# S5 layer of a decoder trunk: recurrence steps issued in two parts, and five small pieces of work put at other places

## The chip, the core and the metric

The kernel runs on one core of a Trainium2 chip. Five engines of that core work side by side and meet at semaphores: TensorE (PE in the profile, with its weight loads as PEld), VectorE (DVE), ScalarE (ACT), GpSimd (POOL) and SyncE (SP), which here only issues transfers from HBM. The metric is the time of one execution in microseconds (us); before the change it was 2031.78 us, the median of 3 runs that lay between 2030.18 and 2032.72 us. One further execution was recorded by the profiler; every duration below comes from that one.

## What is computed

A two-layer decoder trunk in float32 over 256 tokens of width 2048. Layer 0 mixes tokens with an S5 state-space mixer, layer 1 with sliding-window attention; a SwiGLU feed-forward network follows each. The change lies in layer 0's mixer alone:

```python
def s5_mixer(u, a_re, a_im, log_step, b_re, b_im, c_re, c_im, d_skip, w_glu):
    dt = exp(log_step)[:, None]
    lb = exp((a_re + i a_im) * dt)                 # 128 groups x 64 complex states
    q  = (lb - 1) / (a_re + i a_im)
    bb = q[..., None] * (b_re + i b_im)            # 64 states x 16 channels per group
    bu = einsum('lgc,gpc->lgp', u, bb)
    s[l] = lb * s[l-1] + bu[l]                     # the recurrence, over 256 tokens
    y = real(einsum('lgp,gcp->lgc', s, c)) + d_skip * u
    g = gelu(y)
    gl = g @ w_glu                                 # 2048 x 4096
    return gl[..., :2048] * sigmoid(gl[..., 2048:])
```

Its input `u` is the RMS norm of `x` with weights `norm_mix[0]`.

## The kernel before, in words

**Tiling.** The 256 tokens are cut into 64 chunks (`NK`) of 4 tokens (`L`). Inside a chunk the effect of the tokens on each other is a small matrix product on TensorE (`own_tokens`, with the matrices `M`); from chunk to chunk runs the recurrence, 63 values of the state, so 62 steps. The 128 groups form 64 pairs; pairs are split in two halves `hf` = 0 and 1, each with its own state tile `V0` or `V1` (`V` in the profile) of 64 chunks x 64 numbers per partition (real and imaginary parts of 32 columns). The two recurrences don't depend on each other.

**Ahead of the recurrence** (the first 56 us of the profile), TensorE and ScalarE go back and forth: `turned_x` transposes a block of `X` (TensorE, `px`) and ScalarE copies it (`xt`); `tokens` does the same with the normed input (`pu`, `U`); `added` multiplies both (`pv`), and `kept` copies the product into `V0` or `V1` on ScalarE. Blocks are numbered (t, b) with t = 0 to 3, b = 0 to 3; t = 0, 1 fill `V0`, and t = 2, 3 fill `V1`. The norm needs its weights spread over the partitions: two matrix products `gb` with `sel`; they are used by `scaled` (tile `xs`), which VectorE computes after the norm's scale `r` is known. The sum of squares behind `r` passes TensorE as the product `rb`. `pl` is another small set of products shortly before it (the powers of lb, by pair).

**The recurrence.** `step(hf)` is three VectorE instructions: a product of 4 x 32 numbers per partition (line 573) and two sums of 2 x 32 (lines 576 and 578), each on what the one before wrote. Early steps of half 0 are called by `lead`; the main loop (line 851 on) then calls a step of half 0 and, once `reached[0]` is more than `LEAD` = 20 ahead, one of half 1. When half 0 is through, half 1 goes on alone by `more`. ScalarE copies finished states into `St`, in cuts that end at chunks 28, 52, 60 and 64.

**After the recurrence.** `outputs(q)` (line 798) multiplies the states `St[q]` and adds them to `own_tokens(q)` (line 776) in the banks `py`; ScalarE applies GELU (`activated`, line 806), TensorE transposes (`turned`, tile `pt`), ScalarE rounds to the high part (line 820) and VectorE subtracts for the low part (line 821) of the tile `gt`. Quarters q = 0 and 2 belong to half 0, and 1 and 3 to half 1. `end(0, 2)` and `end(1, 3)` do this for two quarters.

**The weights.** `w_glu` and all later matrices come as pieces of 512 x 512 numbers, 1 MB, loaded by SyncE's queue into `raw`, of which there are two buffers. `W.high(i)` makes the rounded high part on ScalarE (line 122), `W.low(i)` the rest, on VectorE (line 127) unless GpSimd is named. A raw buffer is free for piece i+2 once both parts of piece i are made. A piece takes 24 products on TensorE (lines 922 to 924: high x high, low, and low x high, for 4 row blocks and 2 token blocks). `early_piece` runs the first four pieces between the S5 stages.

**What sets the order.** Each engine takes its instructions in one fixed order. Calls wrapped in `pin`, and the calls between `V.on = True` and `V.on = False` for that engine, stay in the order in which the program is written; the others are placed by a scheduler when the program is built. Waits on semaphores are inserted at the same time, wherever an instruction reads or overwrites what another one writes. They are tracked by stretches of memory, so a wait may stand between two instructions whose numbers interleave but are not the same.

Of the kernel before, what the change touches and what calls it, by code (L numbers as in the profile page):

```python
# [9 lines left out]
F32 = mybir.dt.float32  # L10
# [7 lines left out]
P = 128  # L18
# [29 lines left out]
def bc(ap, axis, n):  # L48

    v = ap.unsqueeze(axis)  # L50
    shape = list(v.shape)
    shape[axis] = n
    return v.to_broadcast(shape)
# [3 lines left out]
def kernel(  # L57
# [22 lines left out]
    def bank(shape, name="ps"):  # L80
        return ps.tile(shape, F32, tag="ps", name=nm(name))
# [112 lines left out]
    def s5(early_piece):  # L194
# [3 lines left out]
        with st:  # L198
# [21 lines left out]
            def rows(g2):  # L220
                return slice(g2 * NS, (g2 + 1) * NS)
# [70 lines left out]
            S.copy(Bn[:, 2], Bn[:, 0])  # L292


            gb = [bank([P, 512], "gb") for _ in range(2)]
            for hf in range(2):
                PE.matmul(gb[hf], sel.rearrange("p k h -> p (k h)"), nrow[:, 512 * hf : 512 * hf + 512],
                          start=True, stop=True)


            V.on = False
            n_small = [0]

# [75 lines left out]
            nr, t, u, w = (sp.tile(sh, F32, name=f"q{i}") for i in range(4))  # L379
            V.on = True  # L380
            V.tensor_scalar(nr, LP[:, 0, 0], -1.0, None, ALU.add)
            PL.tensor_tensor(u, LP[:, 0, 1], aim, op=ALU.mult)
            PL.tensor_tensor(t, nr, are, op=ALU.mult)
            PL.tensor_tensor(w, nr, aim, op=ALU.mult)
            PL.tensor_tensor(t, t, u, op=ALU.add)
            PL.tensor_tensor(u, LP[:, 0, 1], are, op=ALU.mult)
            PL.tensor_tensor(q_[:, 0], t, iv, op=ALU.mult)
            PL.tensor_tensor(u, u, w, op=ALU.subtract)
            PL.tensor_tensor(q_[:, 1], u, iv, op=ALU.mult)


            ssq = sp.tile([P, L], F32, name="ssq")

# [6 lines left out]
            def turned_b(o, i, evict):  # L400
                f = 0 if o is B1 else 1
                b = Bn[:, f : f + 2].rearrange("p r s c -> p (r s) c")
                pt = bank([P, 4, G])
                for c in range(4):
                    PE.transpose(pt[:, c], b[:, :, 4 * i + c], ident)
                evict(o[:, :, 4 * i : 4 * i + 4], pt.rearrange("p c g -> p g c"))
# [9 lines left out]
            turned_b(B1, 3, S.copy)  # L416
            turned_b(B2, 0, negated)
            squares(2)
            turned_b(B2, 1, negated)
            for i in (2, 3):  # L420
                turned_b(B2, i, lambda o, v: V.tensor_scalar(o, v, sgn[:, 1:2], None, ALU.mult))


# [7 lines left out]
            for l in range(L):  # L431
                for ri in range(2):
                    for g2 in range(2):
                        PE.matmul(pl[rows(g2), l, ri], LP[:, l, ri], ident[:, g2::2], start=True, stop=True)
            LRs = sp.tile([P, 3, G], F32, name="LRs")
            S.copy(LRs, LR)

# [11 lines left out]
            def last_token(t):  # L449
                S.copy(X[t][:, :, :, 3].rearrange("p (h a) g c -> p h (a g) c", h=2), of_groups(B1, t))  # L450
# [69 lines left out]

            tokens(0, 0)
            tokens(0, 1)
            last_token(1)

            early.close()
            lp = st.enter_context(tc.tile_pool(name="s5late", bufs=1))
# [2 lines left out]
            def turned_x(t, b):  # L529
                px = bank([P, 4, P], "px")  # L530
                for i in range(4):
                    PE.transpose(px[:, i], X[t][:, 4 * b + i].rearrange("p g j c -> p (g j c)"), ident)
                xt[t, b] = lp.tile([P, 4, 2, NS], F32, tag="xt", name=nm("xt"), bufs=4)
                S.copy(xt[t, b].rearrange("p a r s -> p a (r s)"), px)
# [11 lines left out]
            def kept(t, b, copy):  # L546
                p0 = 16 * (b // 2) + 8 * (t % 2) + 4 * (b % 2)
                copy(Vt[t // 2][:, 1:, :, p0 : p0 + 4], pvs[t, b].rearrange("p r a k -> p k r a")[:, : NK - 1])
# [14 lines left out]
            def step(hf, parts=1, keep=lambda ins: ins):  # L563

                reached[hf] += 1
                k = reached[hf]
                n = 32 // parts
                ws, pr = scan[hf][:, 0], scan[hf][:, 1]
                vs = []
                for i in range(parts):  # L570
                    part = slice(n * i, n * (i + 1))
                    t_ = pr[..., part]
                    keep(V.tensor_tensor(t_, ws[..., part], bc(Vt[hf][:, k - 1, :, part], 1, 2), op=ALU.mult))  # L573
                    vs.append((Vt[hf][:, k, :, part], t_))
                for v, t_ in vs:
                    V.tensor_tensor(v, v, t_[:, 0], op=ALU.add)  # L576
                for v, t_ in vs:
                    V.tensor_tensor(v, v, t_[:, 1, ::-1], op=ALU.add)  # L578

            def lead(n):  # L580
                for i in range(n):
                    step(0)

            for t in (2, 3):
                real_parts(t)
            PL.tensor_copy(drows[:, :, 3], drow.rearrange("a (g c) -> a g c", g=2))

            def imag_and_tokens(t):
                for j in (2, 1):
                    imag(t, j)  # L590
                for j in (2, 1):
                    token(t, j)
                imag(t, 0)
                token(t, 0)

            turned_x(0, 0)
            turned_x(0, 1)
            imag_and_tokens(1)
            added(0, 0)
            kept(0, 0, S.copy)  # L600
# [36 lines left out]
            PL.tensor_tensor(Cq[:, :, 0], Cq[:, :, 0], c2[:, :, 1], op=ALU.subtract)  # L637
            PL.tensor_tensor(Cq[:, :, 1], Cq[:, :, 1], c2[:, :, 0], op=ALU.add)

            lead(4)  # L640
            last_token(2)
            tokens(2, 0)
# [2 lines left out]
            turned_x(2, 1)  # L645
            added(2, 0)
            kept(2, 0, S.copy)
            turned_x(2, 2)
            added(2, 1)
            kept(2, 1, S.copy)  # L650
# [19 lines left out]
            lead(3)  # L670
            added(3, 2)
            kept(3, 2, S.copy)

            pc = bank([P, PAIRS], "pc")
            PE.transpose(pc, drows.rearrange("a g j c -> a (g j c)"), ident[:PAIRS, :PAIRS])
            dcol = lp.tile([P, PAIRS], F32, name="dcol")
            S.copy(dcol, pc)
            dd = lp.tile([P, PAIRS, GC], F32, name="dd")
            PL.tensor_tensor(dd, bc(dcol, 2, GC), bc(idm, 1, PAIRS), op=ALU.mult)
            added(3, 3)  # L680
            kept(3, 3, S.copy)
            lead(2)
            W.high(0, pin)
            W.low(0, pin, PL)
            for e in (V, S, PL, PE):
                e.on = False

# [163 lines left out]
                    pin(copied(q, cuts[cuts.index(k1) - 1], k1))  # L851

            while reached[0] < NK - 1:
                step(0)
                if reached[0] + 1 in cuts:
                    copies((0, 2), reached[0] + 1)
                if reached[0] + 1 == cuts[2]:

                    M[1] = kernels(lags, pin)
                    for q in (0, 2):  # L860
                        own_tokens(q)
                if reached[1] + LEAD < reached[0] < NK - 1:
                    step(1)
            W.high(1, pin)

            def more(n):

                for i in range(min(n, NK - 1 - reached[1])):
                    step(1, keep=pin)

            rest = cuts[1:]

# [10 lines left out]
            early_piece(gt, 0, 0, last)  # L883
            W.low(2, pin)
            W.high(3, pin)
            W.low(3, pin, PL)
            for q in (1, 3):
                St[q] = big([P, 2, 16, NK], "St")
            copies_so_far()
# [5 lines left out]
            own_tokens(1)  # L895
            W.high(4, pin)
            last = end(1, 3, lambda: own_tokens(3))
            early_piece(gt, 1, 2, last)
            W.low(4, pin)
            W.high(5, pin)  # L900
# [406 lines left out]
```

## Time and profile before

| | |
|---|---|
| median of 3 runs | 2031.78 us (2030.18 to 2032.72) |
| the profiled execution's own time | 2030.9 us |
| its span, first to last instruction | 2029.1 us |
| mean granted TensorE clock | 0.993 of full speed |
| S5's recurrence: half 1's first step starts | 56.55 us |
| half 0's last step is done, half 1 goes on alone | about 98.4 us |
| first `outputs(1)` product, right after half 1's last states | 124.61 us |
| TensorE's idle time after 180 us, in 1849 us | 12.9 us |

The profiled execution is 0.88 us shorter than the median. The span leaves out 1.8 us ahead of and behind the instructions. The first rows of the table show the shape: some 130 us of S5, in which no engine works all the time, and then some 1900 us of products, in which TensorE hardly ever stops. In a row of a timeline the first number is the start in us from the span's start, the second the duration; a bracket gives the idle time just before the row, and what ended it.

### The profile page before, as it was taken

What the parts mean: (1) busy time and instruction counts of PE and PEld (TensorE: products, weight loads), DVE (VectorE), ACT (ScalarE), POOL (GpSimd) and SP (SyncE); (2) the same over time, 40 slices, a digit from 0 to 9 for tenths busy, and PEclk for the clock granted to TensorE, in tenths of its full rate; (3) what the DMA queues carried; (4) which work ended last, traced back from release to release, by engine and by line L of the source; (5) the groups of instructions that cost most, each with busy time, mean ns of one, the idle gap of its engine ahead of it and who ended that gap; (6) DMA issues with size and microseconds to landing.
All of it is one profiled execution on the core that took longest, in us unless ns stands there. A gap on an engine that the chain in (4) does not pass through costs nothing.

```text
span 2029.1 us, 25100 instructions
## 1 busy us (share of the span) xinstructions
PE 1984.3 (98%) x10640; PEld 1638.7 (81%) x10640; DVE 1088.9 (54%) x1343; ACT 860.1 (42%) x871; POOL 103.7 (5%) x77
## 2 busy tenths in 40 slices
PE   7699999999999999999999999999999999999998
PEld 6578888888888888888887778888888888888886
DVE  8955454445544544454567775544454445444445
ACT  6554444443344334333445454544333343334333
POOL 6850000000000000000000000000000000000000
PEclk9899999999999999999999999999999999999999
DMA  4037666565555655556555334556555655555564
GB/s 128 23 111 233 198 198 194 186 194 192 187 188 188 199 193 187 187 192 200 178 191 166 106 125 146 186 188 193 194 192 187 188 191 193 195 186 188 190 201 148
DMA packets 183317, 360.62 MB, mean 178 GB/s; under 512 B 10403, under 2 KB 10467, under 8 KB 183077
## 3 DMA queue, kind: packets, MB, share of 16 engines
q1 hardware_dynamic: 182192, 355.56, 54.4%
q8 instruction: 83, 1.36, 0.3%
q10 hardware_dynamic: 580, 2.14, 0.3%
q0 software_dynamic: 432, 1.33, 0.2%
q14 instruction: 30, 0.24, 0.0%
HBM read 356.90 MB, written 2.10 MB: 177 GB/s over the span
## 4 chain that ended last, share of the span: by engine, by line
PE 91%; DVE 6%; ACT 1%; DMA 1%; issue 1%; POOL 0%; DVEq 0%; ACTq 0%
PE acc L922 29%; PE acc L924 29%; PE acc L923 28%; DVE scan L573 1%; DVE w L127 1%; PE tr L1061 1%; DVE V L578 1%; DVE V L576 1%; DMA raw<-in_s_w_glu_dram 1%; PE pv L210 1%; PE tr L966 1%; PE po L1208 1%; PE tr L1197 0%; PE py L798 0%; ACT sc L1181 0%
## 5 line engine op out<-in xcount | busy, mean ns | idle before, releaser
L127 DVE TENSOR_TENSOR w<-raw,w 128x2048 fp32r<-128x2048 f32 x330 | 757.1, 2295 | 828.3 <-ACT w L122 828.3
L122 ACT ACTIVATE w<-raw 128x2048 fp32r<-128x2048 f32 x332 | 636.2, 1916 | 979.4 <-PE acc L924 873.6
L922 PE MATMUL acc<-w,xT 128*128 128x512 f32 x1568 | 612.8, 391 | 0.0
L924 PE MATMUL acc<-w,xT 128*128 128x512 f32 x1568 | 611.3, 390 | 0.0
L923 PE MATMUL acc<-w,xT 128*128 128x512 f32 x1568 | 610.6, 389 | 0.0
L924 PEld LDWEIGHTS acc<-w,xT 128*128 128x128 f32 x1568 | 294.3, 188 | 62.2 <-issue 1.0
L922 PEld LDWEIGHTS acc<-w,xT 128*128 128x128 f32 x1568 | 294.4, 188 | 61.3 <-issue 1.3
L923 PEld LDWEIGHTS acc<-w,xT 128*128 128x128 f32 x1568 | 294.4, 188 | 60.7 <-issue 0.5
L922 PE MATMUL acc<-w,hT 128*128 128x512 f32 x704 | 275.2, 391 | 0.0
L923 PE MATMUL acc<-w,hT 128*128 128x512 f32 x704 | 273.6, 389 | 0.0
L924 PE MATMUL acc<-w,hT 128*128 128x512 f32 x704 | 273.4, 389 | 0.0
L922 PEld LDWEIGHTS acc<-w,hT 128*128 128x128 f32 x704 | 132.1, 188 | 28.0 <-ACT hT L1063 1.2
L924 PEld LDWEIGHTS acc<-w,hT 128*128 128x128 f32 x704 | 132.1, 188 | 27.8
L923 PEld LDWEIGHTS acc<-w,hT 128*128 128x128 f32 x704 | 132.2, 188 | 27.0
L923 PE MATMUL acc<-w,gt 128*128 128x512 f32 x256 | 99.8, 390 | 0.6 <-DVE w L127 0.6
L922 PE MATMUL acc<-w,gt 128*128 128x512 f32 x256 | 100.1, 392 | 0.0
L924 PE MATMUL acc<-w,gt 128*128 128x512 f32 x256 | 99.7, 389 | 0.0
L923 PEld LDWEIGHTS acc<-w,gt 128*128 128x128 f32 x256 | 48.1, 188 | 10.6 <-DVE w L127 1.0
L924 PEld LDWEIGHTS acc<-w,gt 128*128 128x128 f32 x256 | 48.1, 188 | 10.1
L922 PEld LDWEIGHTS acc<-w,gt 128*128 128x128 f32 x256 | 48.1, 188 | 9.9
L1088 DVE TENSOR_TENSOR h<-h,acc 128x512 f32<-128x512 f32 x64 | 43.3, 686 | 23.7 <-PE acc L924 23.7
L1074 ACT ACTIVATE act<-acc,ry 128x512 f32<-128x512 f32 x44 | 30.1, 690 | 59.9 <-PE acc L924 59.9
(242 smaller groups left out, 1233.1 us busy)
## 6 DMA issues: line engine op xcount, KB each, us to landing
raw<-in_ffn_w_gate_dram SPq DMA_DIRECT2D x88, 1024.0 KB, 5.2
raw<-in_ffn_w_up_dram SPq DMA_DIRECT2D x88, 1024.0 KB, 5.2
raw<-in_ffn_w_down_dram SPq DMA_DIRECT2D x88, 1024.0 KB, 5.1
raw<-in_s_w_glu_dram SPq DMA_DIRECT2D x32, 1024.0 KB, 5.3
raw<-in_attn_w_qkv_dram SPq DMA_DIRECT2D x20, 1024.0 KB, 5.2
raw<-in_attn_w_o_dram SPq DMA_DIRECT2D x16, 1024.0 KB, 5.1
xk<-in_x_dram SPq DMA_DIRECT2D x4, 512.0 KB, 7.4
h<-in_x_dram SPq DMA_DIRECT2D x8, 256.0 KB, 5.6
```

Source lines behind the costliest of these rows:

```text
L122: keep(S.activation(w[:, 0], self.raw[i], AF.Copy))
L127: keep(e.tensor_tensor(lo, self.raw[i], hi.bitcast(F32), op=ALU.subtract))
L210: return (lambda *a, **k: pin(f(*a, **k))) if self.on else f
L573: keep(V.tensor_tensor(t_, ws[..., part], bc(Vt[hf][:, k - 1, :, part], 1, 2), op=ALU.mult))
L576: V.tensor_tensor(v, v, t_[:, 0], op=ALU.add)
L578: V.tensor_tensor(v, v, t_[:, 1, ::-1], op=ALU.add)
L922: keep(PE.matmul(acc, x_[:, 0], w[0][:, a], start=first, stop=False))
L923: PE.matmul(acc, x_[:, 0], w[1][:, a], start=False, stop=False)
L924: PE.matmul(acc, x_[:, 1], w[0][:, a], start=False, stop=last)
L966: PE.transpose(pt[:, t], h[t][:, kt * P : (kt + 1) * P], ident)
L1074: S.activation(s, pg[t], AF.Silu, scale=r[0][:, t : t + 1])
L1088: V.tensor_tensor(hc, hc, acc[t], op=ALU.add)
```

## The change

It has five parts, all in S5:

1. `step` was already written for several `parts`, and now `lead` and `more` ask for two, as does the main loop as long as half 1 hasn't begun. A step in two parts is two products of 4 x 16 numbers, two sums, and two sums more, where there were one, one and one.
2. The products `gb` that spread the norm's weights go from the start to behind `pl`, and the eight GpSimd instructions for `q` go from ahead of the `tmp` products (`real_parts(0)` and `(1)`) to behind them.
3. One transposed block of `B2` (`turned_b(B2, 1)`) is evicted by VectorE and not by ScalarE, and `last_token(1)`, a copy on ScalarE, comes two blocks later.
4. D's column (`pc`, `dcol`, and `dd` on GpSimd) and both parts of weight piece 0 (`W.high(0)` on ScalarE, `W.low(0)` on GpSimd) are written earlier: `dcol` ahead of `lead(4)`, `W.high(0)` behind `kept(2, 0)`, where both had stood near the end of the preparation.
5. `W.low(3)`, the low part of the fourth piece, goes from GpSimd to VectorE, and from ahead of half 1's last steps to behind `end(1, 3)`.

```diff
@@ start of S5
-            gb = [bank([P, 512], "gb") for _ in range(2)]
-            for hf in range(2):
-                PE.matmul(gb[hf], sel.rearrange("p k h -> p (k h)"), nrow[:, 512 * hf : 512 * hf + 512],
-                          start=True, stop=True)
...
             V.tensor_scalar(nr, LP[:, 0, 0], -1.0, None, ALU.add)
-            PL.tensor_tensor(u, LP[:, 0, 1], aim, op=ALU.mult)
...
-            PL.tensor_tensor(q_[:, 1], u, iv, op=ALU.mult)
...
-            turned_b(B2, 1, negated)
-            for i in (2, 3):
+            for i in (1, 2, 3):
                 turned_b(B2, i, lambda o, v: V.tensor_scalar(o, v, sgn[:, 1:2], None, ALU.mult))
...
                         PE.matmul(pl[rows(g2), l, ri], LP[:, l, ri], ident[:, g2::2], start=True, stop=True)
+            gb = [bank([P, 512], "gb") for _ in range(2)]
+            for hf in range(2):
+                PE.matmul(gb[hf], sel.rearrange("p k h -> p (k h)"), nrow[:, 512 * hf : 512 * hf + 512],
+                          start=True, stop=True)
             LRs = sp.tile([P, 3, G], F32, name="LRs")
...
             tokens(0, 1)
-            last_token(1)
...
             def lead(n):
                 for i in range(n):
-                    step(0)
+                    step(0, 2)
+            PL.tensor_tensor(u, LP[:, 0, 1], aim, op=ALU.mult)
...
+            PL.tensor_tensor(q_[:, 1], u, iv, op=ALU.mult)
             for t in (2, 3):
                 real_parts(t)
...
             turned_x(0, 1)
+            last_token(1)
...
+            pc = bank([P, PAIRS], "pc")
+            PE.transpose(pc, drows.rearrange("a g j c -> a (g j c)"), ident[:PAIRS, :PAIRS])
+            dcol = lp.tile([P, PAIRS], F32, name="dcol")
+            S.copy(dcol, pc)
+            dd = lp.tile([P, PAIRS, GC], F32, name="dd")
+            PL.tensor_tensor(dd, bc(dcol, 2, GC), bc(idm, 1, PAIRS), op=ALU.mult)
             lead(4)
...
             kept(2, 0, S.copy)
+            W.high(0, pin)
+            W.low(0, pin, PL)
             turned_x(2, 2)
...
             kept(3, 2, S.copy)
-            pc = bank([P, PAIRS], "pc")
...
-            PL.tensor_tensor(dd, bc(dcol, 2, GC), bc(idm, 1, PAIRS), op=ALU.mult)
             added(3, 3)
             kept(3, 3, S.copy)
             lead(2)
-            W.high(0, pin)
-            W.low(0, pin, PL)
@@ main loop and half 1 alone
             while reached[0] < NK - 1:
-                step(0)
+                step(0, 1 if reached[1] > 1 else 2)
...
             def more(n):
                 for i in range(min(n, NK - 1 - reached[1])):
-                    step(1, keep=pin)
+                    step(1, 2, pin)
...
             W.high(3, pin)
-            W.low(3, pin, PL)
...
             last = end(1, 3, lambda: own_tokens(3))
+            W.low(3, pin)
             early_piece(gt, 1, 2, last)
```

**Where a scheduler decides, the order shows it.** The first place is VectorE where half 1 sets in. `V_77` is half 0's state, `V_78` half 1's; `scan_593` holds half 0's factors and products, `scan_805` and after the change `scan_837` half 1's; a bracket names the semaphore that the instruction waits for (`DVE_49` is VectorE's own), and `x2` stands for two such rows. Before:

```order
L573 TENSOR_TENSOR scan_593<-scan_593,V_77 128x128 [waits DVE_49]
L576 TENSOR_TENSOR V_77<-V_77,scan_593 128x64 [waits DVE_49]
L578 TENSOR_TENSOR V_77<-V_77,scan_593 128x64 [waits DVE_49]
L573 TENSOR_TENSOR scan_593<-scan_593,V_77 128x128 [waits DVE_49]
L573 TENSOR_TENSOR scan_805<-scan_805,V_78 128x128 [waits Activation_49]
L576 TENSOR_TENSOR V_77<-V_77,scan_593 128x64 [waits DVE_49]
L576 TENSOR_TENSOR V_78<-V_78,scan_805 128x64 [waits DVE_49]
L578 TENSOR_TENSOR V_77<-V_77,scan_593 128x64 [waits DVE_49]
L578 TENSOR_TENSOR V_78<-V_78,scan_805 128x64 [waits DVE_49]
```

After the change:

```order
L562 TENSOR_TENSOR scan_593<-scan_593,V_77 128x4x16 [waits DVE_49] x2
L565 TENSOR_TENSOR V_77<-V_77,scan_593 128x2x16 [waits DVE_49]
L565 TENSOR_TENSOR V_77<-V_77,scan_593 128x2x16
L567 TENSOR_TENSOR V_77<-V_77,scan_593 128x2x16 [waits DVE_49] x2
L562 TENSOR_TENSOR scan_837<-scan_837,V_78 128x128 [waits Activation_49]
L562 TENSOR_TENSOR scan_593<-scan_593,V_77 128x4x16 [waits DVE_49]
L565 TENSOR_TENSOR V_78<-V_78,scan_837 128x64 [waits DVE_49]
L562 TENSOR_TENSOR scan_593<-scan_593,V_77 128x4x16 [waits DVE_49]
L567 TENSOR_TENSOR V_78<-V_78,scan_837 128x64 [waits DVE_49]
L565 TENSOR_TENSOR V_77<-V_77,scan_593 128x2x16 [waits DVE_49]
L565 TENSOR_TENSOR V_77<-V_77,scan_593 128x2x16
L567 TENSOR_TENSOR V_77<-V_77,scan_593 128x2x16 [waits DVE_49] x2
```

The first four rows after the change are a step of half 0 in two parts: six instructions, of which the second product waits for the first, the first sum for the second product, and only the second sum of the first pair waits for nothing. Then stands a pair of steps in which half 0 is in two parts and half 1 is whole, nine instructions where there were six. Counted along the engine, half 0 now makes 13 steps ahead of half 1's first (16 before), then there are 8 such mixed pairs, 33 pairs of whole steps (41 whole pairs before), 8 whole steps of half 0 alone (5 before), and 21 steps of half 1 alone, in two parts (21 before, whole).

The second place is ScalarE while it fills `V1`; `V_78` rows are `kept`, `xt` rows `turned_x`. Before, the rows from block (2, 0) on:

```order
L210 COPY xt_695<-px_690 128x512 [waits PE_49]
L210 COPY V_78<-pv_697 128x126x4 [waits PE_49]
L210 COPY xt_720<-px_715 128x512 [waits PE_49]
L210 COPY V_78<-pv_722 128x126x4 [waits PE_49]
L210 COPY xt_745<-px_740 128x512 [waits PE_49,Activation_49]
```

After the change:

```order
L210 COPY xt_713<-px_708 128x512 [waits PE_49]
L210 COPY V_78<-pv_715 128x126x4 [waits PE_49]
L122 ACTIVATE w_735<-raw_733 128x2048 [waits DMAHW0_49]
L210 COPY xt_743<-px_738 128x512 [waits PE_49]
L210 COPY V_78<-pv_745 128x126x4 [waits PE_49]
L210 COPY xt_768<-px_763 128x512 [waits PE_49,Activation_49]
```

Weight piece 0's high part now stands between the copy of block (2, 0) and the transposed block (2, 2); before it stood behind the last copy into `V1`.

The third place is VectorE behind half 1's last step, with the low parts of `gt` (first the tile of quarter 1, then that of quarter 3) and of weight pieces 4, 5 and 6. Before:

```order
L578 TENSOR_TENSOR V_78<-V_78,scan_805 128x64 [waits DVE_49]
L821 TENSOR_TENSOR gt_2119<-pt_2114,gt_2119 128x512 [waits Activation_49]
L821 TENSOR_TENSOR gt_2119<-pt_2122,gt_2119 128x512 [waits Activation_49]
L821 TENSOR_TENSOR gt_2186<-pt_2181,gt_2186 128x512 [waits Activation_49]
L821 TENSOR_TENSOR gt_2186<-pt_2189,gt_2186 128x512 [waits Activation_49]
L127 TENSOR_TENSOR w_176_1976<-raw_1797,w_176_1976 128x2048 [waits DMAHW4_49]
L127 TENSOR_TENSOR w_2209<-raw_1888,w_2209 128x2048 [waits DMAHW5_49,Activation_49]
```

After the change:

```order
L567 TENSOR_TENSOR V_78<-V_78,scan_837 128x2x16 [waits DVE_49] x2
L819 TENSOR_TENSOR gt_2244<-pt_2239,gt_2244 128x512 [waits Activation_49]
L819 TENSOR_TENSOR gt_2244<-pt_2247,gt_2244 128x512 [waits Activation_49]
L127 TENSOR_TENSOR w_1929<-raw_1885,w_1929 128x2048 [waits DMAHW3_49,Pool_49]
L819 TENSOR_TENSOR gt_2312<-pt_2307,gt_2312 128x512 [waits Activation_49]
L819 TENSOR_TENSOR gt_2312<-pt_2315,gt_2312 128x512 [waits Activation_49]
L127 TENSOR_TENSOR w_176_2101<-raw_1887,w_176_2101 128x2048 [waits DMAHW4_49]
```

The low part of piece 3 (`w_1929`) now stands behind the first of the two `gt` tiles, where it can't run before `outputs(1)` and the transposes of quarter 1 are done. SyncE's queue has its loads in the same order as before.

More of the change, by code (lines that the diff above doesn't have):

```diff
@@ L381, in s5 @@
             V.tensor_scalar(nr, LP[:, 0, 0], -1.0, None, ALU.add)
-            PL.tensor_tensor(u, LP[:, 0, 1], aim, op=ALU.mult)
[L383 to L388, printed above, removed]
-            PL.tensor_tensor(q_[:, 1], u, iv, op=ALU.mult)
             ssq = sp.tile([P, L], F32, name="ssq")
@@ L581, in lead @@
                 for i in range(n):
-                    step(0)
+                    step(0, 2)
+            PL.tensor_tensor(u, LP[:, 0, 1], aim, op=ALU.mult)
+            PL.tensor_tensor(t, nr, are, op=ALU.mult)
+            PL.tensor_tensor(w, nr, aim, op=ALU.mult)
+            PL.tensor_tensor(t, t, u, op=ALU.add)
+            PL.tensor_tensor(u, LP[:, 0, 1], are, op=ALU.mult)
+            PL.tensor_tensor(q_[:, 0], t, iv, op=ALU.mult)
+            PL.tensor_tensor(u, u, w, op=ALU.subtract)
+            PL.tensor_tensor(q_[:, 1], u, iv, op=ALU.mult)
             for t in (2, 3):
@@ L672, in s5 @@
             kept(3, 2, S.copy)
-            pc = bank([P, PAIRS], "pc")
[L675 to L678, printed above, removed]
-            PL.tensor_tensor(dd, bc(dcol, 2, GC), bc(idm, 1, PAIRS), op=ALU.mult)
             added(3, 3)
```

## The prediction

> **What bounds the kernel now.** I read first a view that sums the engines' busy time by stretches of the span, cut at the events of S5.
>
> ```profile
> core 0: us, PE busy (x) PEld busy (x) DVE busy (x) ACT busy (x) POOL busy (x), PEclk, DMA share, GB/s
> 0.00:56.55 56.55, 46.14 (x727) 38.79 (x729) 46.36 (x169) 37.01 (x75) 31.62 (x39) 0.94 0.38 115
> 56.55:98.38 41.83, 26.50 (x553) 22.98 (x548) 41.35 (x260) 21.25 (x30) 40.63 (x20) 0.84 0.09 27
> 98.38:124.61 26.23, 24.35 (x409) 20.48 (x409) 22.93 (x70) 19.19 (x25) 24.15 (x8) 1.00 0.28 85
> 124.61:146.90 22.29, 19.19 (x386) 16.24 (x387) 6.98 (x6) 8.41 (x16) 0.00 (x0) 1.00 0.33 109
> 180.00:2029.00 1849.00, 1836.08 (x8432) 1514.06 (x8430) 953.28 (x825) 756.13 (x711) 1.63 (x3) 1.00 0.57 184
> ```
>
> The second column is the stretch's length. After 180 us TensorE is busy for 1836 of 1849 us, so whatever S5 loses or wins ahead of it moves the end by as much. From 56.55 to 98.38, while both halves step, VectorE is busy for 41.35 of 41.83 us: it is the bound. From 98.38 to 124.61, with half 1 alone, VectorE (22.93) and TensorE (24.35) lie close together. So I take four terms: the start of half 1 (E1, now 56.55), the end of half 0 (E2, 98.38), the start of `outputs(1)` (T0, 124.61), and what comes behind T0.
>
> The timeline of VectorE gives a step's price.
>
> ```profile
> 40.72 0.30 DVE L573 TENSOR_TENSOR scan<-scan,V 128x128 f32<-128x128 f32 x1
> 41.05 0.22 DVE L576 TENSOR_TENSOR V<-V,scan 128x64 f32<-128x64 f32 x1
> 41.31 0.22 DVE L578 TENSOR_TENSOR V<-V,scan 128x64 f32<-128x64 f32 x1
> 41.56 0.30 DVE L573 TENSOR_TENSOR scan<-scan,V 128x128 f32<-128x128 f32 x1
> ...
> 56.55 0.30 DVE L573 TENSOR_TENSOR scan<-scan,V 128x128 f32<-128x128 f32 x1 [2.88 <-ACT V L210]
> ...
> 94.28 0.29 DVE L573 TENSOR_TENSOR scan<-scan,V 128x128 f32<-128x128 f32 x1
> ...
> 103.98 1.29 DVE L821 TENSOR_TENSOR gt<-pt,gt 128x512 fp32r<-128x512 f32 x2 [0.57 <-ACT gt L820]
> ...
> 123.80 0.22 DVE L578 TENSOR_TENSOR V<-V,scan 128x64 f32<-128x64 f32 x1
> ```
>
> A step alone takes 41.56 - 40.72 = 0.84 us (0.845 over many steps): 0.33 from the product to its sum, 0.26 and 0.25 from sum to sum and on. The 41 pairs from 56.55 to 94.28 take 37.73, 0.92 each, little more than half of two steps alone: the halves fill each other's waits. Half 1's first product waits 2.88 us for ScalarE's last copy into `V1`, so E1 belongs to the preparation, not to VectorE.
>
> **Part 1: steps in two parts.** What I need is the distance from start to start with a wait on the instruction just before, and without one.
>
> ```profile
> 11.54 0.22 DVE L369 TENSOR_TENSOR LP<-LP 128x64 f32<-128x64 f32 x1
> 11.68 0.22 DVE L370 TENSOR_TENSOR cm<-LP 128x64 f32<-128x64 f32 x1
> ...
> 18.52 0.17 DVE L210 TENSOR_TENSOR rb<-rb,r 128x4 f32<-128x4 f32 x1
> 18.72 0.17 DVE L210 SCALAR_TENSOR_TENSOR rb<-rb,r 128x4 f32<-128x4 f32 x1
> ```
>
> Two neighbours of 64 elements that don't need each other stand 0.14 apart (11.54 to 11.68); in the steps above 64 elements with a wait take 0.255. With 4 elements a waiting neighbour still comes 0.20 later (18.52 to 18.72). So halving an instruction saves little of the wait. For 32 elements, which the trace doesn't have, I estimate 0.22 with a wait (between 0.20 and 0.255) and 0.10 without (0.14 for 64; half of it, 0.07, is the least). By the order above, a two-part step alone is: first product, then the second, which waits for it (0.255); first sum, which waits for the second product (0.255); its neighbour, unwaiting (0.10); then the two second sums, each waiting for its own first sum, whose 0.22 runs from that sum's start, so 0.12 and 0.10; and 0.22 until the last is done and the next product may start. Sum: 0.255 + 0.255 + 0.10 + 0.12 + 0.10 + 0.22 = **1.05 to 1.06 us**, against 0.845: 0.215 dearer. The gain that was there to be had, a second part running in the first one's wait, is lost where the second product waits for the first.
>
> A mixed pair has nine instructions. Issued without a stop they take 0.20 (128 elements; 0.40 for the two of a whole pair, of 0.92) + 4 x 0.135 (64) + 4 x 0.10 (32) = 1.14; I take 1.16, 0.235 more than 0.925.
>
> From E1 to E2 there were 41 pairs and 5 steps; now there are 8 mixed pairs, 33 pairs and 8 steps (3 more, because only 13 stand ahead): 8 x 0.235 + 3 x 0.845 = **+4.4 us**. The 13 two-part steps ahead of E1 are 13 x 1.06 = 14 us from about 40, done at 54 and before E1, so they cost nothing. From E2 to T0, 21 steps alone are 0.215 dearer: 4.5. Of that, 0.57 lies in the wait at 103.98 for `gt`, so **+4.0**. VectorE's last sum at 123.80, then ScalarE's copy, then T0 is the chain there, and it gets later by this.
>
> **Parts 2 and 4: the start of half 1.** The timelines of TensorE, VectorE and ScalarE (the engine stands in each row):
>
> ```profile
> 3.13 3.75 PE L210 MATMUL gb<-nrow,sel 2*128 2x512 f32 x4 [3.13 <-DVE sm L310]
> 14.78 1.11 PE L210 MATMUL pl<-ident,LP 128*64 128x64 f32 x32
> 16.38 0.39 PE L210 MATMUL rb<-ssq,both 128*128 128x4 f32 x2 [0.49 <-ACT U L210]
> ...
> 17.46 0.16 DVE L210 TENSOR_SCALAR rb<-rb 128x4 f32<-128x4 f32 x1
> ...
> 68.00 1.46 PE L754 MATMUL pm<-k,shift 128*128 128x256 f32 x6
> ...
> 42.61 0.58 ACT L210 COPY V<-pv 128x504 f32<-128x504 f32 x1 [0.76 <-PE pv L210]
> 43.19 0.59 ACT L210 COPY xt<-px 128x512 f32<-128x512 f32 x1
> ...
> 44.75 1.15 PE L210 MATMUL pv<-U,xt 64*64 64x64 f32 x32
> ...
> 54.54 0.27 PE L210 MATMUL pc<-ident,drows 64*128 64x64 f32 x1
> ...
> 56.42 1.92 ACT L122 ACTIVATE w<-raw 128x2048 fp32r<-128x2048 f32 x1
> ```
>
> `gb` now stands between `pl`, which ends at 15.89, and `rb`. At 3.13 its four matmuls took 3.75. Later 128x256 ones take 1.46 / 6 = 0.24, so twice the width gives 0.49 and 1.9 for four; I take 1.9, since TensorE has been running since 13.4 us. Then `rb` runs from 17.8 to 18.2 and the norm's first VectorE instruction comes at 18.2 for 17.46: +0.8, down to -0.5 if the lighter ScalarE and GpSimd queues (0.7 us of `B2`, eight `q` of 0.3) move the whole front up, up to +2.6 at 3.75.
>
> `W.high(0)`, 1.92 us, goes between the rows 42.61 and 43.19 of ScalarE. The `xt` copy then ends at 43.19 + 0.59 + 1.92 = 45.70, and the product that takes it stood at 44.75: +0.95. Later waits of ScalarE give some back; I take +0.8, with 0 and 1.9 as ends. `pc` goes from the last stretch of that chain (0.2 off) to an earlier one (0.15 on). The other moves lie under waits: `dd` and `W.low(0)` on an idle GpSimd, the `B2` block on VectorE ahead of a norm that is later anyway. **E1: +1.5 us.**
>
> **Part 5 and what follows T0.** The timelines of TensorE, VectorE and GpSimd, and a row of the page's list of transfers:
>
> ```profile
> 124.61 2.10 PE L798 MATMUL py<-T,St 64*64 64x64 f32 x128 [0.17 <-ACT St L785]
> 126.49 1.14 PE L776 MATMUL py<-M,U 64*64 64x64 f32 x64
> 127.43 0.28 PE L798 MATMUL py<-T,St 64*64 64x64 f32 x3
> 129.78 1.15 PE L798 MATMUL py<-T,St 64*64 64x64 f32 x61 [2.08 <-issue]
> ...
> 133.75 0.50 PE L922 MATMUL acc<-w,gt 128*128 128x512 f32 x1
> ...
> 141.40 0.50 PE L923 MATMUL acc<-w,gt 128*128 128x512 f32 x1 [0.57 <-DVE w L127]
> ...
> 132.18 1.29 DVE L821 TENSOR_TENSOR gt<-pt,gt 128x512 fp32r<-128x512 f32 x2 [8.16 <-ACT gt L820]
> 139.06 4.48 DVE L127 TENSOR_TENSOR w<-raw,w 128x2048 fp32r<-128x2048 f32 x2
> ...
> 118.36 4.63 POOL L127 TENSOR_TENSOR w<-raw,w 128x2048 fp32r<-128x2048 f32 x1
> ...
> raw<-in_s_w_glu_dram SPq DMA_DIRECT2D x32, 1024.0 KB, 5.3
> ```
>
> `W.low(3)` leaves GpSimd, where its 4.63 us ended before T0 and delayed nobody, and takes 4.48 / 2 = 2.24 on VectorE, behind the first `gt`. That ended at 132.18 + 1.29, 8.9 behind T0, and piece 3 began at 133.75, 9.1 behind. TensorE has some own tokens of quarter 3 done sooner (-0.8), and the 2.08 at 129.78, in which nothing but "issue" holds it, may go, as the next weight load, which ran just then, starts only after `W.low(3)`. Without these 2.9 us `gt` is ready 6.0 behind T0, and `W.low(3)` ends at 8.4; piece 3's second product waits for it. So most of the gain is eaten: piece 3 in earnest at 8.4 to 9 for 9.1, and piece 4's low part, queued behind, costs up to 0.95 for the 0.57 at 141.40; some further products fit into the wait. I take **-1.3**, with -2.7 and +1 as ends.
>
> Sum: 1.5 + 4.4 + 4.0 - 1.3 = **+8.6 us**. The profiled execution's own time was 2030.9 us, 0.9 below the median: 2039.5 by the one, 2040.4 by the other. I forecast **2040.0**.
>
> **The rivals.**
>
> *The parts cost nothing (not slower; 0.14).* The place is VectorE's waits between parts. If an instruction costs by its elements, and a wait for the one just before it is nothing, then 32 elements take 0.07, a mixed pair 0.20 + 0.54 + 0.28 = 1.02, so 8 of them +0.8, and a two-part step alone 0.27 + 0.28 = 0.55. Half 1 alone is then TensorE's matter: its pieces end 0.2 before T0 already, and own tokens put ahead add 0.8. Sum: 1.5 + 0.8 + 2.5 + 0.8 - 1.3 = +4.3, about 2035.2, within 0.2% of 2031.78 (that is within 4.06 us, about what a measurement of this kernel can tell from no change), and faster only if E1 and the tail come out at their low ends. It decides from a two-part step of some 0.85 down. The rows speak against it: 0.26 from 41.05 to 41.31 with a wait, 0.14 from 11.54 to 11.68 without one, both of 64 elements. The Trainium skill, "VectorE: DVE Perf Modes", section "The DRAIN you can't avoid", speaks for it: eight copies with a semaphore after each took as long as eight with one at the end, "the semaphore costs nothing extra here". By that rule the two-part step would be no dearer for its waits; the trace disagrees, with 0.14 and 0.26.
>
> *`gb` at the slow price (0.13).* It takes 3.75 between `pl` and `rb`, as at 3.13, and E1 is 1.8 later still: +10.4, about 2041.8. For it speaks that TensorE's work before 17 us is in short bursts with waits; against it, that `pl` and `LR` just before ran.
>
> *The tail turns into a wait for weights (0.15).* The raw buffer of piece 3 is free only after `W.low(3)`, 8.4 us behind T0 rather than before T0, so piece 5's load starts that much later. With 5.3 us of load and some 4.2 of high and low part it is ready 17.9 behind T0. TensorE reaches it at 8.4 + 2 x 5.3 + 1 = 20.0 (a piece is 24 products of 0.22, 1836 us by 8432 instructions; 1 for the last transposes). That leaves 2 us; if load and parts take longer than that, the tail is +1 and the sum +10.9, about 2042.3.
>
> **How the numbers follow.** The forecast has 0.58, the rivals 0.14, 0.13 and 0.15. I give 0.04 to faster by over 0.2%, 0.10 to within 0.2%, both out of the first rival and the low ends of E1 and tail; all else, 0.86, is slower by over 0.2%. The range goes from 2034.5 (just under the first rival) to 2043 (the tail's rival with some of `gb`'s).
>
> **What would show each step.** In the profile after: two-part steps alone 1.05 us apart (0.85 or less, and the first rival holds); mixed pairs 1.16; half 1's first product near 58.0; its last sum near 133.7; `W.low(3)` on VectorE ahead of a waiting product of piece 3; no 2 us of "issue" behind T0. I am wrong if a wait that I read in the order is passed without delay, or if TensorE or the weights take up more than 4 us of the delay behind T0.

## The result, and the profile after

| | before | after |
|---|---|---|
| median of 5 runs | 2031.59 us (2030.18 to 2032.72) | 2039.74 us (2038.61 to 2040.99) |
| ratio | | 1.0041, 95% interval 1.0026 to 1.0056 |
| the profiled execution's own time | 2030.9 us | 2038.61 us |
| its span | 2029.1 us | 2036.8 us |

The change makes the kernel slower by 8.15 us, 0.4%. Of the executions reported further down, one of the run whole (3347.78 us) and one of sbuf_apart (2237.74 us) ran at a far lower granted clock (0.556 and 0.845) than the others (0.98 and more); the medians count them and the ratios leave them out.

The time by stretches after, cut at the same events as before; the second column is the length:

```profile
0.00:56.60 56.60, 43.26 (x727) 37.24 (x728) 47.27 (x199) 37.84 (x74) 36.77 (x40) 0.94 0.45 133
56.60:103.08 46.48, 31.47 (x531) 26.74 (x529) 45.65 (x295) 19.55 (x29) 43.32 (x21) 0.74 0.01 2
103.08:132.65 29.57, 26.70 (x480) 22.21 (x473) 27.00 (x133) 19.23 (x26) 7.35 (x4) 1.00 0.24 73
188.00:2036.80 1848.80, 1835.79 (x8431) 1513.78 (x8429) 952.48 (x825) 756.03 (x710) 1.63 (x3) 1.00 0.57 184
```

Set against the cuts of before, the loss lies in two stretches and nowhere else. From half 1's start to half 0's end: 46.48 for 41.83, +4.65. From there to `outputs(1)`: 29.57 for 26.23, +3.34. The start is where it was (56.60 for 56.55), and what follows `outputs(1)` takes 2036.80 - 132.65 = 1904.15 for 1904.49, -0.34. The sum, 7.70, is the difference of the two spans. The last row is what it was (TensorE busy for 1835.8 of 1848.8 us, 1836.1 of 1849.0 before): the long stretch of products takes no part.

VectorE's timeline after, at the places that were shown of before:

```profile
41.04 0.50 DVE L562 TENSOR_TENSOR scan<-scan,V 128x64 f32<-128x64 f32 x2
41.58 0.28 DVE L565 TENSOR_TENSOR V<-V,scan 128x32 f32<-128x32 f32 x2
41.80 0.29 DVE L567 TENSOR_TENSOR V<-V,scan 128x32 f32<-128x32 f32 x2
42.12 0.50 DVE L562 TENSOR_TENSOR scan<-scan,V 128x64 f32<-128x64 f32 x2
...
56.60 0.43 DVE L562 TENSOR_TENSOR scan<-scan,V 128x128 f32<-128x128 f32 x2 [2.70 <-ACT V L210]
...
57.76 0.42 DVE L562 TENSOR_TENSOR scan<-scan,V 128x128 f32<-128x128 f32 x2
...
65.81 0.49 DVE L562 TENSOR_TENSOR scan<-scan,V 128x128 f32<-128x128 f32 x2
...
117.10 2.28 DVE L127 TENSOR_TENSOR w<-raw,w 128x2048 fp32r<-128x2048 f32 x1
```

A two-part step alone takes 42.12 - 41.04 = 1.08 us (0.845 whole). Its two products take 0.54, from 41.04 to the first sum at 41.58: two full waits, one behind the other. The four sums take the other 0.54. A mixed pair takes (65.81 - 56.60) / 8 = 1.15 (0.92 whole). Half 1's first product waits for ScalarE as before, now 2.70 us.

### The profile page after: what moved, and what is told of

Its sections match the earlier page's. It is cut to its first block, busy times and chain, and to the rows that moved or that the text cites. A ratio compares the mean times of both kernels' runs of the same rounds, so it can differ in the third digit from the quotient of the medians.

```text
span 2036.8 us, 25226 instructions
## 1 busy us (share of the span) xinstructions
PE 1989.9 (98%) x10640; PEld 1643.4 (81%) x10640; DVE 1100.2 (54%) x1471; ACT 859.6 (42%) x870; POOL 96.4 (5%) x76
## 4 chain that ended last, share of the span: by engine, by line
PE 91%; DVE 6%; DMA 1%; ACT 1%; issue 0%; SPq 0%; DVEq 0%; ACTq 0%
PE acc L922 28%; PE acc L920 28%; PE acc L921 28%; DVE scan L562 2%; DVE w L127 1%; DVE V L565 1%; DVE V L567 1%; PE tr L1059 1%; DMA raw<-in_s_w_glu_dram 1%; PE pv L210 1%; PE tr L964 1%; PE po L1206 1%; PE tr L1195 0%; ACT sc L1179 0%; ACT w L122 0%
```

## Experiments

Twelve kernels, each measured beside the kernel before on the same chip; medians, ratios with 95% intervals. E1 is half 1's first product, T0 the first product of `outputs(1)`, tail the span from T0 to the end, all in the profiled execution.

| run | median us | ratio to before | E1 | T0 | tail |
|---|---|---|---|---|---|
| kernel before | 2031.3 to 2032.0 | | 56.55 | 124.61 | 1904.5 |
| the change | 2039.74 | 1.0041 (1.0026 to 1.0056) | 56.60 | 132.65 | 1904.2 |
| whole | 2032.31 | 1.0002 (0.9993 to 1.0011) | 57.11 | 125.68 | 1904.8 |
| parts_only | 2037.47 | 1.0029 (1.0018 to 1.0041) | 57.03 | 135.31 | 1902.3 |
| low3_only | 2031.76 | 0.9999 (0.9990 to 1.0008) | 56.48 | 124.42 | 1904.0 |
| sbuf_apart | 2071.83 | 1.0181 (1.0162 to 1.0200) | | | |
| psum_lead | 2027.91 | 0.9982 (0.9973 to 0.9990) | 57.67 | 121.47 | 1904.7 |
| psum_both | 2028.46 | 0.9985 (0.9977 to 0.9994) | 58.40 | 123.43 | 1903.6 |
| low3_pool | 2036.63 | 1.0025 (1.0015 to 1.0036) | 56.43 | 132.35 | 1900.6 |
| more_whole | 2036.36 | 1.0024 (1.0014 to 1.0035) | 57.78 | 131.08 | 1903.6 |
| gb_only | 2031.84 | 0.9998 (0.9989 to 1.0007) | 56.94 | 126.86 | 1903.5 |
| high0_only | 2031.14 | 0.9998 (0.9988 to 1.0007) | 57.85 | 125.93 | 1902.7 |
| lead_apart_only | 2030.99 | 0.9997 (0.9988 to 1.0006) | 56.88 | 124.09 | 1905.0 |
| lead_gb_first | 2027.25 | 0.9975 (0.9965 to 0.9984) | 56.76 | 120.35 | 1904.8 |

### Is it the parts, or the moved work?

**whole**: the changed kernel with one part everywhere.

```diff
-                    step(0, 2)
+                    step(0)
...
-                step(0, 1 if reached[1] > 1 else 2)
+                step(0)
...
-                    step(1, 2, pin)
+                    step(1, 1, pin)
```

> The changed kernel with every step of the recurrence in one part again, all else as changed. Theory (the parts cost the time): the alone step is 0.845 us again, half 1 starts near 56.6, half 0 ends near 98.0, outputs(1) starts near 124.5; what remains is the start (0) and the tail (-0.3), so about 2031.3 us, within 1 us of the kernel before. Rival (the moved pieces of work cost it): 2036 or more.

Measured 2032.31, no difference to before that can be measured. The parts cost 7.4 us of the change; for all the moved work together 0.4 is left by the ratio, 0.7 by the medians, and at most 2.2 (the upper end of the interval).

**parts_only**: the kernel before with the two-part steps and nothing else (the same three edits, the other way round).

> The kernel before with the two-part steps alone, none of the moved work. By the order half 0 makes 12 two-part steps ahead, then 9 mixed pairs, 32 pairs and 9 whole steps, then half 1 alone for 21 in two parts. Theory: from half 1's start to half 0's end 9 x 0.23 + 4 x 0.845 = +5.5, half 1 alone +3.4, no gain behind outputs(1): about 2040.4 us, at least as slow as the whole change. Rival (the parts are half of it and the moved work the other half): 2035 to 2037.

Measured 2037.47, a miss of 2.9 us, nearer to the rival than to the theory. In its profile, which is 1.9 above its median, T0 is even later than the theory has it, 10.7 after before's for 8.9. What the theory missed is the tail, 2.2 us shorter: TensorE, waiting longer for half 1, did work of later ahead of `outputs(1)`. So the parts alone cost 5.9, and with the moved work 7.4. The intervals don't resolve this difference of 1.5, but the tail of the change is not shorter (1904.2), as if something in the moved work turned bad beside the parts. The next two runs look for it.

**low3_only**: the kernel before with part 5 alone (`W.low(3, pin)` behind `end(1, 3, ...)`).

> The kernel before with only W.low(3) on VectorE behind end(1, 3). Theory: outputs(1) starts at 124.6 as before; behind it the stall of 2.1 us in outputs(3) is gone, and piece 3's second product waits for W.low(3) instead, so the rest gets shorter by 0.3 us (0 to 1.3): about 2031.3 us. Rival (the later load of piece 5 becomes a wait): a wait for weights after piece 4 and 2032.5 or more.

2031.76: nothing either way, as the theory had it. **low3_pool**: the changed kernel without part 5.

```diff
             W.high(3, pin)
+            W.low(3, pin, PL)
...
-            W.low(3, pin)
```

> The changed kernel with W.low(3) back on GpSimd ahead of half 1's steps. Theory (with the parts, TensorE has more of its own tokens done ahead and then waits for W.low(3) on VectorE, which the kernel with the parts alone didn't): the rest behind outputs(1) is 1902.3 us as there and not 1904.2, so about 2037.9 us. Rival (the low part on VectorE costs nothing): 2039.7 us.

2036.63, 3.1 below the change. Beside the two-part steps part 5 is dear; without them it costs nothing. TensorE's timeline ahead of T0 in low3_pool:

```profile
127.14 2.09 PE L774 MATMUL py<-M,U 64*64 64x64 f32 x96
129.16 0.50 PE L920 MATMUL acc<-w,gt 128*128 128x512 f32 x1
129.49 0.39 PE L921 MATMUL acc<-w,gt 128*128 128x512 f32 x1
...
131.78 0.39 PE L922 MATMUL acc<-w,gt 128*128 128x512 f32 x1
132.10 0.44 PE L774 MATMUL py<-M,U 64*64 64x64 f32 x6
132.35 2.09 PE L796 MATMUL py<-T,St 64*64 64x64 f32 x128
```

And in the change, where the low part of piece 3 isn't made yet:

```profile
127.73 2.09 PE L774 MATMUL py<-M,U 64*64 64x64 f32 x96
129.75 0.73 PE L920 MATMUL acc<-w,gt 128*128 128x512 f32 x2
132.22 0.32 PE L774 MATMUL py<-M,U 64*64 64x64 f32 x2 [1.73 <-DVE V L567]
132.65 2.69 PE L796 MATMUL py<-T,St 64*64 64x64 f32 x128
...
142.95 0.50 PE L921 MATMUL acc<-w,gt 128*128 128x512 f32 x1 [0.74 <-DVE w L127]
```

In low3_pool TensorE fills the wait for half 1's last state with 12 products of piece 3. In the change it can do only the two that need high parts alone and stands for 1.73 us. Piece 3 then still waits 0.74 for its low part. Between the two TensorE's clock is low: `outputs(1)` takes 2.69 for 2.09, and the sum over the stretch behind T0 has a mean granted clock (the third number from the end) of 0.73:

```profile
132.65:139.00 6.35, 6.35 (x230) 6.23 (x230) 0.00 (x0) 3.41 (x7) 0.00 (x0) 0.73 0.02 5
```

That the standing still brought the low clock is not shown. In the run lead_apart_only a wait of 3.42 us ahead of `outputs(1)` is followed by a low clock too (3.09 for 2.09, further down), but in the run whole one of 1.83 us at this place is not (1.00 from 125.68 to 132.00).

### Which of the two kinds of steps

**more_whole**: the changed kernel with half 1's steps alone whole again (`step(1, 1, pin)`).

> The changed kernel with half 1 alone in whole steps; half 0 keeps its two-part steps and the mixed pairs. Theory: half 0 still ends near 103.1; half 1 alone takes 26.2 to 26.9 us for 29.6, outputs(1) near 129.6, the rest is 0 to 1 us longer: about 2037 us. Rival (TensorE binds there): outputs(1) stays near 132 and the time at 2039.5.

2036.36, 3.4 below the change, as the theory has it: half 1 alone in two parts costs about 3.4, and the rest of the parts' price lies ahead of it. The 3.1 of low3_pool and these 3.4 may be partly the same: with half 1 sooner, the wait of 1.73 us that low3_pool fills with products is gone from TensorE's rows. No run has both.

### Why a two-part step is dear

**sbuf_apart**: the changed kernel with the two parts' products in two tiles of SBUF.

```diff
+            prods = [[sp.tile([P, 2, 2, 16], F32, name=f"pr{hf}{i}") for i in range(2)] for hf in range(2)]
...
-                    t_ = pr[..., part]
+                    t_ = prods[hf][i] if parts == 2 else pr[..., part]
```

> The changed kernel with the products of a two-part step in two tiles of SBUF, one for each part, so that nothing of one part waits for the other; in the order 22 two-part steps of half 0 now stand ahead of half 1's first, then 40 whole pairs, then half 1 alone for 22. Theory (a two-part step is dear because its second product waits for the first): the six instructions fill each other's waits and the step alone takes about 0.70 us; 22 of them end before 56.6, the pairs take 37 us, half 1 alone is bound by TensorE at some 27.4 us after half 0's end; outputs(1) near 121.5 and about 2028.3 us, faster than both kernels. Rival (six instructions with a wait each cost more than three, whoever they wait for): a step alone stays at 1.0 us or more, half 1 starts near 62 and the time is 2040 or more.

2071.83: the theory's time is missed by 43 us, and by its time alone the run would speak for the rival. VectorE's timeline shows that it doesn't:

```profile
46.76 4.48 DVE L568 TENSOR_TENSOR V<-V,pr 128x32 f32<-128x32 f32 x1
51.16 0.18 DVE L566 TENSOR_TENSOR V<-V,pr 128x32 f32<-128x32 f32 x1
...
51.64 0.22 DVE L563 TENSOR_TENSOR pr<-scan,V 128x64 f32<-128x64 f32 x1
51.77 0.18 DVE L568 TENSOR_TENSOR V<-V,pr 128x32 f32<-128x32 f32 x1
51.89 0.19 DVE L566 TENSOR_TENSOR V<-V,pr 128x32 f32<-128x32 f32 x1
52.00 0.22 DVE L563 TENSOR_TENSOR pr<-scan,V 128x64 f32<-128x64 f32 x1
```

GpSimd's timeline of the same run:

```profile
46.65 4.54 POOL L210 TENSOR_TENSOR w<-raw,w 128x2048 fp32r<-128x2048 f32 x1 [0.48 <-ACT w L122]
60.65 2.04 POOL L716 TENSOR_TENSOR tmpT<-Cg,LPT 128x1024 f32<-128x1024 f32 x1 [9.46 <-DVE V L568]
```

With the products in SBUF each sum reads two SBUF operands, and a sum that meets a running GpSimd instruction lasts until that one ends: 4.48 us beside the 4.54 of `W.low(0)`, for a sum of 0.18. (The Trainium skill, "SBUF — State Buffer", section "Who interferes with whom", says that a VectorE instruction with two SBUF inputs contends with a GpSimd instruction that reads SBUF, and calls the pair of ports that they share an exclusive lock; the run agrees, with 4.48 us for 0.18, and the expectation should have reckoned with it.) In the stretch in which GpSimd rests, 51.2 to 60.6, one part follows the other every 0.36 us (51.64, 52.00): a two-part step takes **0.72**, six instructions that each wait, though for one that isn't the nearest.

**psum_lead**: the same separation, in two PSUM banks, so that a sum reads one operand from SBUF; half 1 alone in whole steps.

```diff
+            apart += [bank([P, 2, 2, 16], "pr") for _ in range(2)]
...
-                    t_ = pr[..., part]
+                    t_ = apart[i] if parts == 2 else pr[..., part]
...
-                    step(1, 2, pin)
+                    step(1, 1, pin)
```

> The changed kernel with the two products of a two-part step of half 0 in two PSUM banks of their own (no second SBUF operand), half 1 alone in whole steps. In the order 21 two-part steps stand ahead of half 1's first, then 41 whole pairs, none alone. Theory (the false wait between the parts is the price of a two-part step): alone 0.72 us, as in the undisturbed stretch of the run with SBUF tiles, with no stalls beside GpSimd; 21 of them end by 55; half 1 starts at 56.6 and half 0 ends near 94.4, 4 us sooner than before; outputs(1) near 121.8, about 2028.8 us, faster than both kernels. Rival 1 (the earlier run was slow for its order and not for its SBUF operand): steps alone or the start of half 1 are as late as there, 2050 or more. Rival 2 (the end is set by TensorE's and ScalarE's work, not by half 0's end): outputs(1) stays at 124 and the time at 2031.

```profile
42.00 0.36 DVE L562 TENSOR_TENSOR pr<-scan,V 128x64 f32<-128x64 f32 x2
42.27 0.31 DVE L565 TENSOR_TENSOR V<-V,pr 128x32 f32<-128x32 f32 x2
42.50 0.30 DVE L567 TENSOR_TENSOR V<-V,pr 128x32 f32<-128x32 f32 x2
42.72 0.36 DVE L562 TENSOR_TENSOR pr<-scan,V 128x64 f32<-128x64 f32 x2
...
57.67 0.50 DVE L562 TENSOR_TENSOR scan<-scan,V 128x128 f32<-128x128 f32 x2 [2.66 <-ACT V L210]
...
95.59 0.29 DVE L562 TENSOR_TENSOR scan<-scan,V 128x128 f32<-128x128 f32 x1
```

2027.91, faster than both kernels. The step takes 0.72, with the products 0.27 apart from the first sum instead of 0.54. Since the order is made by a scheduler, the wait that is gone also changes the order: 21 steps (16 before, 13 in the change) stand ahead of half 1's first, none is left over at the end, and from E1 to half 1 alone it takes 95.59 - 57.67 = 37.9 us for 41.8.

One thing about the wait can be read from the order of the change. In `V` the numbers of the two parts interleave in SBUF just as the two products interleave in their bank, and yet the second sum waits for nothing there. So interleaving alone doesn't bring the wait. What this run takes away is the common PSUM bank; whether two products in stretches of one bank that don't interleave would do as well, no run shows.

**psum_both**: half 1 alone in two parts on the same banks as well.

> As the run before it in this list, and half 1's 21 steps alone in two parts as well, on the same two banks. Theory: a step alone 0.72 for 0.845, but TensorE reaches outputs(1) no sooner than 27.4 us after half 0's end, so outputs(1) comes 0 to 1 us sooner than with whole steps: about 2028.3 us. Rival: it is VectorE that binds there, and 21 x 0.12 = 2.6 us come off: 2026.2.

2028.46, no difference to psum_lead that these intervals resolve. Half 1's last state comes 61.7 us after E1 (63.2 in psum_lead), but T0 65.0 after E1 (63.8 there): VectorE is done sooner, and TensorE, busy with pieces and own tokens without a gap up to T0, isn't ready for it. The rival that VectorE binds there (2026.2) is out; the gain of up to 1 us that the theory allowed isn't seen.

### The moved work by itself

**lead_apart_only**: the kernel before with psum_lead's steps of half 0, and none of the moved work.

> The kernel before with only half 0's steps ahead of half 1 in two parts whose products lie in two PSUM banks of their own; none of the moved work. Theory: half 0 ends near 94.4 as in psum_lead, but GpSimd ends its T products only at 118 and W.low(3) at 123, and ScalarE's copies of half 1's states (7.7 us) wait for them, so outputs(1) starts at 123 to 124.5 and the time is 2030 to 2031 us: the gain needs dd and W.low(0) off GpSimd's late stretch. Rival (GpSimd doesn't bind): outputs(1) at 121 and 2027.9 us, as psum_lead.

2030.99 with T0 at 124.09, as the theory has it. ScalarE's, TensorE's and GpSimd's rows:

```profile
116.10 8.16 ACT L786 COPY St<-V 128x896 f32<-128x896 f32 x8 [3.54 <-POOL tmpT L718]
...
124.09 3.09 PE L799 MATMUL py<-T,St 64*64 64x64 f32 x128 [3.42 <-ACT St L786]
...
114.03 2.04 POOL L718 TENSOR_TENSOR tmpT<-Cg,LPT 128x1024 f32<-128x1024 f32 x1
116.14 2.41 POOL L723 TENSOR_TENSOR T<-T,tmpT 128x1024 f32<-128x1024 f32 x1
```

ScalarE's copies of half 1 start only when GpSimd has ended with a tile of its T products (114.03 + 2.04; they make the matrices by which `outputs` multiplies the states), and `outputs(1)` waits 3.42 us for them. So the moved work earns nothing while half 0 is slow, and about 3 us (2030.99 to psum_lead's 2027.91) once it is faster. By these rows that is GpSimd's part of it; no run moves that part alone.

**gb_only** and **high0_only**: the kernel before with `gb` behind `pl`, and with `W.high(0)` and `W.low(0)` behind `kept(2, 0)`.

> The kernel before with only the two products gb behind pl. Theory: gb takes 1.98 us there and rb waits for it, so the first pu of TensorE starts LR's start plus 7.5 to 8.1 us and follows every shift of the transposes ahead of it (20.8 to 22.2 us in the seven profiles with gb moved, 20.93 to 20.97 in the three without); half 1 starts at 56.2 to 57.4; about 2032 us, within 1 us of before. Rival (the front has gained, since gb no longer holds up the first transposes): pu at 20.3 and 2031 us.

> The kernel before with only W.high(0) and W.low(0) behind the copy of block (2, 0). Theory: the product that takes the xt copy starts 0.8 us later against the one ahead of it, half 1 starts near 57.3, GpSimd ends its T products about 2.6 us sooner; about 2032.3 us. Rival (ScalarE's later waits absorb it): half 1 at 56.5, 2031.5 us.

Neither median tells the theories apart (2031.84, 2031.14); the traces do. In gb_only:

```profile
13.38 0.88 PE L210 MATMUL LR<-ident,LP 128*64 128x128 f32 x12
...
15.78 1.98 PE L210 MATMUL gb<-nrow,sel 2*128 2x512 f32 x4
17.68 0.39 PE L210 MATMUL rb<-ssq,both 128*128 128x4 f32 x2
21.52 1.09 PE L210 MATMUL pu<-ident,xs 128*128 128x128 f32 x4 [3.45 <-DVE xs L210]
```

`rb` follows `gb` without a gap, and the first `pu` comes 8.1 us after `LR` starts; in the change that is 20.92 - 12.77, the same 8.15. High0_only has E1 at 57.85, and GpSimd's T products end 5.2 us sooner (113.2 for 118.4), twice what the theory says; the wait that part 4 makes stands in it and in the change alike, 0.71 us ahead of the product that takes the late `xt` copy:

```profile
46.04 1.15 PE L210 MATMUL pv<-U,xt 64*64 64x64 f32 x32 [0.71 <-ACT xt L210]
```

**lead_gb_first**: psum_lead with `gb` at the start again.

> psum_lead with gb at the start again, as in the kernel before. Theory: the first pu at 20.95 in place of 21.6, half 1 at 57.0 in place of 57.7, so about 2027.4 us, less than the measurement can tell from psum_lead, and faster than both kernels. Rival: gb at the start delays the transposes and the time is 2028.5 or more.

2027.25, ratio 0.9975 (0.9965 to 0.9984) to before: the lowest median of all, though not told apart from psum_lead. Either is a version to keep.

## Why the prediction was right

2040.0 was forecast, 2039.74 measured, and the mechanism is the one named. By its steps, in the profiled execution:

- **A two-part step 1.05 to 1.06, a mixed pair 1.16**: 1.08 and 1.15. The reading that decides, that the second product waits for the first at full price, is shown by psum_lead, where that wait is gone and the step takes 0.72.
- **E1 to E2, +4.4**: +4.65.
- **E2 to T0, +4.0**: +3.34. The steps cost what was said, but `W.low(2)` took 2.28 (117.10 above) where it had taken 2.86 before:

```profile
111.15 2.86 DVE L127 TENSOR_TENSOR w<-raw,w 128x2048 fp32r<-128x2048 f32 x1
```

In the change GpSimd's T products were over by then (110.7, and 118.4 before), since part 4 sent them off earlier and the slower steps bring `W.low(2)` later; in parts_only, without part 4, it took 2.28 too. That I hadn't counted.
- **E1, +1.5**: +0.05 in the profile, and that is the term that was mis-sized. `gb` took 1.98 where 1.9 was said, and `W.high(0)` holds the chain up by its 0.7 to 0.8. But I set them against a front that stood still, and in the profiled execution it was 0.64 earlier (`LR` at 12.77 for 13.41). The six profiles with all of the changed front ahead of E1 have it at 56.43 to 58.40, mean 57.3; the four with the front of before at 56.48 to 57.03, mean 56.7. So +0.6 is nearer, and the profiled execution of the change, 1.1 below its median, was a lucky one.
- **Behind T0, -1.3**: -0.34. Piece 3 waits for `W.low(3)` as said. The 2.1 us of "issue" is gone too, but the runs don't show that as the work of part 5: this idle time is as long with part 5 (0.74 in low3_only, 0.98 in whole) as without it (0.74 in high0_only, 1.01 in gb_only), the 2.08 that I read is the longest of all the profiles, and only the change, with its low clock just there, has none. What else the step missed is ahead of T0: with half 1 late, TensorE has time for piece 3, and part 5 takes the low part away that it needs (low3_pool, 3.1 us).

The errors were -1.45, +0.25, -0.66 and +0.96, together -0.90, and the median lies 1.1 above the profiled execution. That it came within 0.3 us of the forecast is luck; the single terms were off by up to 1.5. The rival by which parts cost nothing falls with the first row; that of `gb` at 3.75 with its 1.98; that of a wait for weights behind piece 4 with the tail, which got no longer, and with TensorE's rows: from T0 to 175 us its only waits over 0.4 are 0.74 and 0.83, both for a low part on VectorE and none for a load. The Trainium skill's "the semaphore costs nothing extra here" ("VectorE: DVE Perf Modes", section "The DRAIN you can't avoid") doesn't hold for instructions as short as these: a pair of products takes 0.50 where the second waits for the first, and 0.36 in psum_lead where it doesn't; a single one takes 0.23, so they start 0.27 and 0.13 apart.

## What to carry to other kernels

Work that is cut in two to fill its own waits gains only if the halves really don't wait for each other: look in the order at what each wait is for, and put what the halves write into separate memory, PSUM banks here, before judging the idea. Under a scheduler such a wait costs twice, in the step and in the order that is built around it. And before work is moved off an idle engine onto the one that feeds the next stage, ask what it fed while the next stage had to wait.

## What the runs showed of the hardware that wasn't expected

A VectorE sum of 0.18 us with two SBUF operands lasted 4.48 us beside a GpSimd instruction of 4.54. The same meeting stretches the weights' low part, whose operands both lie in SBUF. It takes 2.28 us alone; VectorE's timeline of the run whole, in which GpSimd is still at its T products, has

```profile
104.58 3.97 DVE L127 TENSOR_TENSOR w<-raw,w 128x2048 fp32r<-128x2048 f32 x1
...
112.08 3.01 DVE L127 TENSOR_TENSOR w<-raw,w 128x2048 fp32r<-128x2048 f32 x1
```

In the kernel before, where VectorE's low part started first (at 105.18, GpSimd's tile at 105.21), it took its 2.28, and GpSimd's instruction 4.18 for 2.04.

The first 32 transposes of the kernel, the same in every run, took between 5.09 and 6.65 us from profile to profile. With `gb` at the start a wait absorbs this: the first `pu` starts between 20.67 and 20.97 in six profiles. With `gb` on the path nothing does: between 20.84 and 22.20 in eight. Why the transposes vary, and how much of the spread from run to run comes from there, stays open.
